# Two divisions of work moved off VectorE in a two-layer hybrid trunk: softmax scaling to ScalarE, the carried residual's gain and bias to GpSimd

## The chip, the cores and the metric

The kernel runs on one core of a Trainium2 chip. The metric is the device time of one execution in microseconds, median over runs. Of the core's engines, TensorE does matrix products into PSUM, VectorE (DVE in the profile), ScalarE (ACT) and GpSimd (POOL) do elementwise work, and SyncE (SP) issues most of the loads.

## What is computed

Two layers of a mixer with three parallel head groups over 256 tokens of width 2048, cut from the reference:

```python
h = x @ w_in                                     # one projection for all groups
y_a = chunk_band_attention(a_q, a_k, a_v, rel)   # 8 heads, softmax over a band of chunks
o_b = gla_chunk_recurrence(b_q, b_k, b_v, log_g) # 4 heads of gated linear attention
y_m = memory_attention(m_q, mk, mv)              # 4 heads, softmax over 256 memory tokens
y = concat([y_a * silu(a_z), rmsnorm(o_b) * silu(b_z), y_m * silu(m_z)])
x = layer_norm(ALPHA * x + y @ w_out, ln_g, ln_b)
# layer_norm: (x - mean) * rsqrt(var + eps) * ln_g + ln_b, over the 2048 columns
# softmax: exp(s - max) / sum
```

## The kernel before

All weights are streamed from memory, 512 KB at a time, and each product is made nearly exact in float32 by splitting both factors into a high and a low part: ScalarE casts a loaded tile to its high part (`high`, line 261, tile `wh`), VectorE subtracts that from the tile to get the low part (`low`, line 268, tile `wl`), and TensorE multiplies high by high, high by low and low by high (line 86). `take` runs casts three tiles and subtractions two tiles ahead of the tile that TensorE uses; `wh` has four buffers and `wl` three, so the two engines often wait for TensorE to let go of one.

The order of the work is set in two ways. TensorE and SyncE run in the order in which the program is written. ScalarE, VectorE and GpSimd are put in order by a scheduler ahead of the run, from its own estimates of when each step is ready; each engine then runs its list strictly in that order, waiting where it must. Casts and subtractions of weights carry a high priority there.

The heads are generators that run beside the weight stream. After every weight tile `tick` advances them, at most two heads at a time; a number yielded says after how many ticks the next step is written. So TensorE's part of a head (scores, transposes, products) stands at a fixed place between its weight tiles, whatever the other engines do.

- `a_head` (band attention, 8 heads a layer, in pairs): scores, bias, row maximum (line 718), exponential with the row sum as a by-product (line 720, ScalarE), reciprocal of the sum (line 722), then the scaling of the 128 x 384 scores in two pieces, 128 and 256 wide (line 724, in place, VectorE). Three ticks later TensorE transposes them (line 729).
- `m_head` (cross-attention, 4 heads a layer, in pairs 0 and 1, 2 and 3): the same with two pieces of 256; maximum at lines 753 and 754, exponential at 757, reciprocal at 760, scaling at 762, transposes two ticks later at 767.
- `gla` (the gated group) runs beside the first band heads. Its end is copied from PSUM (line 677), squared and summed (684), its root taken (504), scaled (690) and transposed (696).
- `norm_residual(l)` runs in layer 1 beside the stage of the gates. Between the layers `norm_between` leaves the normed values in `res` without gain and bias, since those are put on the transposed copy that feeds the products (line 828). `norm_residual` puts them on `res` itself, which is the residual of layer 1: for each of four column blocks SyncE loads a row of g and a row of b, spread over 128 partitions (line 841), and four operations of 128 x 512 multiply by g and add b for both token tiles (line 844). The rows lie in the same ring of eight scratch buffers as the scores, and SyncE's row loads stand among its weight loads.

In the stage of the gates each half of a group ends with `total` (lines 494 and 495), the gate's SiLU (1107), the product with the group's output (1109), differences of blocks (410 to 413) and splits (498 and 499).

GpSimd fills a few constants and issues small loads, among them the rows for the last norm (lines 797 and 798).

Of the kernel before, what the change touches and what calls it, by code (L numbers as in the profile page):

```python
# [13 lines left out]
ALU = mybir.AluOpType  # L14
# [38 lines left out]
def hybrid_trunk_kernel(  # L53
# [7 lines left out]
    pe, dve, act, pool, sp = nc.tensor, nc.vector, nc.scalar, nc.gpsimd, nc.sync  # L61
# [23 lines left out]
    def mm(o, l, r, start, stop):  # L85
        pe.matmul(o, l, r, start=start, stop=stop, skip_group_check=True)  # L86

    def scratch(shape, dtype=F32):
        return sc.tile(shape, dtype, name=nm("sc"), tag="sc")

    def small(shape, tag, bufs=1):
        return sm.tile(shape, F32, name=nm(tag), tag=tag, bufs=bufs)
# [33 lines left out]
    def banks(n):  # L126
        while len(free) < n:
            yield 1
        return [free.pop(0) for _ in range(n)]

    def release(*bs):
        free.extend(bs)
# [364 lines left out]
    def parts(hi, lo, src):  # L497
        act.copy(hi, src)  # L498
        dve.tensor_tensor(lo, src, hi.bitcast(F32), op=ALU.subtract)  # L499
# [205 lines left out]
    def a_head(h, load_bias, bias, q, k, asv, y):  # L705
        if h + 2 < 8:
            load_bias(h + 2)
        pb, = yield from banks(1)
        mm(ps[:, pb, 0:128], q[:, 0:128], k[:, 0:128], True, True)
        mm(ps[:, pb, 128:384], q[:, 128:256], k, True, True)  # L710
        s = scratch([P, 384])
        dve.scalar_tensor_tensor(s, ps[:, pb, :384], SCALE, bias[h], op0=ALU.mult, op1=ALU.add)
        release(pb)
        mx = small([P, 2], "mx", 4)
        zs = small([P, 2], "zs", 4)
        own = (slice(0, 128), slice(128, 384))
        for t in range(2):
            dve.tensor_reduce(mx[:, t:t + 1], s[:, own[t]], AX.X, ALU.max, negate=True)  # L718
        for t in range(2):
            act.activation(s[:, own[t]], s[:, own[t]], AF.Exp, bias=mx[:, t:t + 1], accum_out=zs[:, t:t + 1])  # L720
        yield 1
        dve.reciprocal(zs, zs)
        for t in range(2):
            dve.tensor_scalar(s[:, own[t]], s[:, own[t]], zs[:, t:t + 1], None, op0=ALU.mult)
        yield 3

        pt, = yield from banks(1)
        for i in range(3):
            pe.transpose(ps[:, pt, i * P:(i + 1) * P], s[:, i * P:(i + 1) * P], ident)  # L729
        pT = scratch([P, 384])  # L730
        act.copy(pT, ps[:, pt, :384])
        release(pt)
        yield 2
        po, = yield from banks(1)
        v0 = 528 + h * P
        mm(ps[:, po, 0:256], asv[:, 0, v0:v0 + P], pT[:, 0:256], True, False)
        mm(ps[:, po, 128:256], asv[:, 1, v0:v0 + P], pT[:, 256:384], False, True)
        act.copy(y, ps[:, po, :256])
        release(po)
        yield 1  # L740

    def m_head(h, q, mk, mv, y):
        pb, = yield from banks(1)
        for t in range(2):
            o = ps[:, pb, t * 256:(t + 1) * 256]
            qh, ql = (x[:, h, t * P:(t + 1) * P] for x in q)
            kh, kl = (x[:, h] for x in mk)
            mm(o, qh, kh, True, False)
            mm(o, ql, kh, False, False)
            mm(o, qh, kl, False, True)  # L750
        mx = small([P, 2], "mx", 4)
        zs = small([P, 2], "zs", 4)
        dve.tensor_reduce(mx, ps[:, pb].rearrange("p (t m) -> p t m", t=2), AX.X, ALU.max, negate=True)
        dve.tensor_scalar(mx, mx, SCALE, None, op0=ALU.mult)
        s = scratch([P, 2, 256])
        for t in range(2):
            act.activation(s[:, t], ps[:, pb, t * 256:(t + 1) * 256], AF.Exp, bias=mx[:, t:t + 1], scale=SCALE, accum_out=zs[:, t:t + 1])
        release(pb)
        yield 1
        dve.reciprocal(zs, zs)  # L760
        for t in range(2):
            dve.tensor_scalar(s[:, t], s[:, t], zs[:, t:t + 1], None, op0=ALU.mult)
        yield 2
        pt, = yield from banks(1)
        for m in range(2):
            for t in range(2):
                pe.transpose(ps[:, pt, m * 256 + t * P:m * 256 + (t + 1) * P], s[:, t, m * P:(m + 1) * P], ident)  # L767
        ph, pl = scratch([P, 2, 256], F32R), scratch([P, 2, 256], F32R)
        parts(ph, pl, ps[:, pt].rearrange("p (m t) -> p m t", m=2))
        release(pt)  # L770
        yield 2
        po, = yield from banks(1)
        for m in range(2):
            vh, vl = (x[:, m, h * P:(h + 1) * P] for x in mv)
            mm(ps[:, po, 0:256], vh, ph[:, m], m == 0, False)
            mm(ps[:, po, 0:256], vl, ph[:, m], False, False)
            mm(ps[:, po, 0:256], vh, pl[:, m], False, m == 1)
        act.copy(y, ps[:, po, :256])
        release(po)
        yield 1  # L780
# [3 lines left out]
    def columns(n):  # L784
        return slice(n * 512, (n + 1) * 512)
# [51 lines left out]
    def norm_residual(l):  # L837
        for n in range(4):
            for a, op in ((ln_g, ALU.mult), (ln_b, ALU.add)):
                row = scratch([P, 512])  # L840
                sp.dma_start(row, a[l:l + 1, columns(n)].to_broadcast([P, 512]))
                for t in range(2):
                    r = res[:, t, columns(n)]
                    dve.tensor_tensor(r, r, row, op=op)
            yield 6

    def norm_vectors():
# [118 lines left out]
    for l in range(L):  # L966
# [82 lines left out]
        def load_bias(h):  # L1049
            bias[h] = hd.tile([P, 384], F32, name=nm("bias"), tag="bias", bufs=3)  # L1050
            sp.dma_start(bias[h], relw[l, h])

        def add_heads(i):
            q, k = qk[i * 2:i * 2 + 2]
            gens.append([a_head(i * 4 + h, load_bias, bias, q[:, h], k[:, h], asv, yraw[1 + i][:, h]) for h in range(4)])
            waiting.extend(gens[-1])
# [27 lines left out]
        if l:  # L1084
            others = [norm_residual(l - 1)]
            beside(others)
        gens.append([m_head(h, q, mk, mv, yraw[3][:, h]) for h in range(4)])
        waiting.extend(gens[-1])

# [65 lines left out]
    with tc.manual_schedule(engines={mybir.EngineType.DVE}):  # L1155
# [6 lines left out]
        for h in range(2):  # L1162
            for kt in range(12, 16):
                moving(ps[:, 6 + h, :256], 1, [columned(v, kt % 2, True, h) for v in ws[kt // 2]], yq[3], kt % 4, kt == 12, kt == 15)
            r = res[:, 1, 1536 + h * 256:1792 + h * 256]
# [93 lines left out]
```

## Time and profile before

| | |
|---|---|
| median of 3 runs | 915.19 us (914.28 to 916.26) |
| profiled execution | 915.43 us, span 913.6 us |
| granted TensorE clock | 0.997 |
| busy: TensorE, VectorE, ScalarE, GpSimd | 904.7, 719.0, 552.4, 13.6 us |
| moved from memory | 193.16 MB read, 214 GB/s over the span |

Times in the profile are microseconds from the start of the span; in groups the mean is in nanoseconds. A row of a group ends with the idle time of the engine just before its instructions and with what ended most of it. In the timeline, consecutive instructions of a kind are merged into one row with their count. Consecutive operations on one engine overlap a little, so the spacing of starts is shorter than the time of one. TensorE's weight loads (PEld) run beside its products.

### The profile page before, as it was taken

How to read it: one execution, taken by the hardware profiler on the slowest of the kernel's cores; microseconds unless marked ns; L12 is line 12 of the kernel's file. 1: busy time of each engine (PE TensorE's matmuls, PEld its weight loads, DVE VectorE, ACT ScalarE, POOL GpSimd, SP SyncE). 2: the span in 40 equal slices, each digit the busy share in tenths (PEclk: the TensorE clock that was granted, in tenths of full speed). 3: DMA queues.
4: the chain of work that ended last, by engine and by line, in shares of the span. 5: the costliest groups of instructions: out<-in, count | busy, mean ns of one | idle time of the engine just before them, and what ended most of it. 6: DMA issues, size and time to landing. Idle time of an engine off the chain costs nothing.

```text
span 913.6 us, 14539 instructions
## 1 busy us (share of the span) xinstructions
PE 904.7 (99%) x5477; PEld 794.8 (87%) x5477; DVE 719.0 (79%) x997; ACT 552.4 (60%) x809; POOL 13.6 (1%) x32
## 2 busy tenths in 40 slices
PE   8999999999999999999999999999999999999997
PEld 6889999999888888788888899999988888888885
DVE  6597788788766777799978867886886778778996
ACT  6575555576576775655559755556756667565540
POOL 1000000000000000000000000000000000100000
PEclk9999999999999999999999999999999999999998
DMA  8858786776444455876765697666754565877652
GB/s 280 301 189 270 271 274 209 233 250 187 156 150 161 161 162 185 300 272 211 230 229 187 203 292 251 222 199 180 222 177 134 182 187 185 277 273 242 218 188 93
DMA packets 65014, 196.21 MB, mean 215 GB/s; under 512 B 7088, under 2 KB 10288, under 8 KB 64944
## 3 DMA queue, kind: packets, MB, share of 16 engines
q1 hardware_dynamic: 63920, 193.08, 64.2%
q0 software_dynamic: 1024, 2.21, 0.8%
q8 instruction: 43, 0.70, 0.3%
q14 instruction: 27, 0.22, 0.1%
HBM read 193.16 MB, written 2.10 MB: 214 GB/s over the span
## 4 chain that ended last, share of the span: by engine, by line
PE 94%; DVE 2%; DMA 1%; ACT 1%; issue 1%; SPq 0%; ACTq 0%; DVEq 0%
PE ps L86 93%; DMA raw<-w 1%; DVE wl L268 1%; PE ps L729 1%; PE ps L767 0%; ACT sz L828 0%; ACT wh L261 0%; DVE x L499 0%; SPq L352 0%; DVE res L812 0%; PE ps L696 0%; SPq L347 0%; DVE s L499 0%; ACT s L498 0%; DVE raw L410 0%
## 5 line engine op out<-in xcount | busy, mean ns | idle before, releaser
L268 DVE TENSOR_TENSOR wl<-raw,wh 128x1024 fp32r<-128x1024 f32 (+1 forms) x313 | 364.6, 1167 | 117.7 <-PE ps L86 78.4
L261 ACT CAST wh<-raw 128x1024 fp32r<-128x1024 f32 (+1 forms) x313 | 314.1, 1008 | 229.6 <-PE ps L86 123.6
L86 PE MATMUL ps<-x,wh 128*128 128x512 f32 x1408 | 445.4, 397 | 0.1
L86 PEld LDWEIGHTS ps<-x,wl 128*128 128x128 f32 x1408 | 264.4, 188 | 63.1 <-DVE wl L268 1.0
L86 PE MATMUL ps<-x,wl 128*128 128x256 f32 x1408 | 277.4, 278 | 0.5 <-DVE wl L268 0.5
L86 PE MATMUL ps<-wh,x 128*128 128x512 f32 (+1 forms) x852 | 247.4, 371 | 1.1 <-DVE sz L495 0.6
L86 PEld LDWEIGHTS ps<-x,wh 128*128 128x128 f32 x1408 | 219.2, 189 | 2.1 <-ACT sz L828 0.4
L86 PEld LDWEIGHTS ps<-wh,x 128*128 128x128 f32 x852 | 155.5, 189 | 21.1 <-ACT wh L358 1.1
L86 PE MATMUL ps<-wl,x 128*128 128x512 f32 (+1 forms) x426 | 157.8, 370 | 0.0
L86 PEld LDWEIGHTS ps<-wl,x 128*128 128x128 f32 x426 | 80.2, 188 | 10.7 <-DVE wl L359 0.4
L261 ACT CAST wh<-term 128x776 fp32r<-128x776 f32 (+1 forms) x39 | 36.0, 924 | 49.2 <-DVE term L260 42.0
L268 DVE TENSOR_TENSOR wl<-term,wh 128x776 fp32r<-128x776 f32 (+1 forms) x39 | 41.5, 1065 | 15.2 <-PE ps L86 14.6
L260 DVE TENSOR_TENSOR term<-term,term 128x776 f32<-128x776 f32 (+1 forms) x39 | 41.3, 1059 | 0.0
L86 PE MATMUL ps<-wh,s 128*128 128x512 f32 (+1 forms) x144 | 41.2, 367 | 0.0
L86 PEld LDWEIGHTS ps<-wh,s 128*128 128x128 f32 x144 | 25.8, 188 | 3.2
L86 PE MATMUL ps<-wl,s 128*128 128x512 f32 (+1 forms) x72 | 26.5, 368 | 0.0
L495 DVE SCALAR_TENSOR_TENSOR sz<-ps,sz 128x512 f32<-128x512 f32 x24 | 16.3, 684 | 4.3 <-ACT sz L494 3.5
L720 ACT ACTIVATE sc<-sc,mx 128x128 f32<-128x128 f32 (+1 forms) x32 | 14.2, 444 | 8.2 <-DVE mx L718 8.2
L86 PE MATMUL ps<-wh,sc 128*128 128x388 f32 x64 | 16.5, 338 | 0.0
L86 PEld LDWEIGHTS ps<-wl,s 128*128 128x128 f32 x72 | 13.5, 188 | 1.6
L1107 ACT ACTIVATE sz<-sz 128x512 f32<-128x512 f32 x16 | 10.1, 632 | 7.4 <-DVE sz L495 7.3
L86 PE MATMUL ps<-w,x 128*128 128x512 f32 (+1 forms) x72 | 14.4, 358 | 0.0
(221 smaller groups left out, 710.6 us busy)
## 6 DMA issues: line engine op xcount, KB each, us to landing
raw<-w SPq DMA_DIRECT2D x252, 512.0 KB, 4.3
raw<-w SPq DMA_DIRECT2D x64, 388.0 KB, 3.6
term<-w SPq DMA_DIRECT2D x24, 388.0 KB, 4.4
term<-w SPq DMA_DIRECT2D x15, 512.0 KB, 4.7
bias<-relw SPq DMA_DIRECT2D x16, 192.0 KB, 3.8
res<-xT SPq DMA_DIRECT2D x4, 512.0 KB, 6.4
res<-xn SPq DMA_DIRECT2D x4, 512.0 KB, 4.8
raw<-memT SPq DMA_DIRECT2D x4, 512.0 KB, 4.8
```

The lines of the kernel that those rows point to most:

```text
L86: pe.matmul(o, l, r, start=start, stop=stop, skip_group_check=True)
L260: in_order(dve.tensor_tensor(d.raw, d.raw, d.plus, op=ALU.add))
L261: act.copy(d.hi, d.raw)
L268: in_order(dve.tensor_tensor(d.lo, d.raw, d.hi.bitcast(F32), op=ALU.subtract))
L495: dve.scalar_tensor_tensor(dst, a, scale, dst, op0=ALU.mult, op1=ALU.add)
L720: act.activation(s[:, own[t]], s[:, own[t]], AF.Exp, bias=mx[:, t:t + 1], accum_out=zs[:, t:t + 1])
L729: pe.transpose(ps[:, pt, i * P:(i + 1) * P], s[:, i * P:(i + 1) * P], ident)
L1107: act.activation(sz, sz, AF.Silu)
```

## The change

Three edits. The scaling of the softmax, lines 724 and 762, becomes a ScalarE multiply by a per-partition factor, with the same operands in place; the reciprocals stay on VectorE. The gain and bias of the carried residual, line 844, go to GpSimd. Over the two layers that is 32 and 16 scalings, and 16 row operations of layer 1.

```diff
@@ a_head @@
         dve.reciprocal(zs, zs)
         for t in range(2):
-            dve.tensor_scalar(s[:, own[t]], s[:, own[t]], zs[:, t:t + 1], None, op0=ALU.mult)
+            act.mul(s[:, own[t]], s[:, own[t]], zs[:, t:t + 1])
         yield 3
@@ m_head @@
         dve.reciprocal(zs, zs)
         for t in range(2):
-            dve.tensor_scalar(s[:, t], s[:, t], zs[:, t:t + 1], None, op0=ALU.mult)
+            act.mul(s[:, t], s[:, t], zs[:, t:t + 1])
         yield 2
@@ norm_residual @@
                 for t in range(2):
                     r = res[:, t, columns(n)]
-                    dve.tensor_tensor(r, r, row, op=op)
+                    pool.tensor_tensor(r, r, row, op=op)
             yield 6
```

The lists of TensorE and SyncE are the same before and after. The scheduler places the moved steps, and shifts some of their neighbours, on the other three engines.

On ScalarE, at cross-attention heads 0 and 1 of layer 0 (`sc_3037` is head 0's scores, `sc_3050` head 1's, `zs` their sums; `wh` are weight casts, `s_3253` and `s_3254` splits of differences):

```order
 L261 CAST wh_3081<-raw_2980 128x1024
 L757 ACTIVATE sc_3050,zs_3047<-ps,mx_3046 128x256 x2
+L762 ACTIVATE sc_3037<-sc_3037,zs_3034 128x256 x2
 L498 CAST s_3253<-raw_3255 128x512
 L498 CAST s_3254<-raw_3255 128x256 x2
 L261 CAST wh_3103<-raw_3009 128x1024
+L762 ACTIVATE sc_3050<-sc_3050,zs_3047 128x256 x2
 L261 CAST wh_3146<-raw_3057 128x1024
 L494 ACTIVATE sz_3125<-ps 128x512
```

Two scalings of head 0 now stand ahead of the splits; the two of head 1 stand behind the splits and one more weight cast.

On ScalarE, at heads 2 and 3 of layer 0 (`sc_3276` and `sc_3289`):

```order
 L757 ACTIVATE sc_3289,zs_3286<-ps,mx_3285 128x256 x2
 L261 CAST wh_3320<-raw_3208 128x1024
+L762 ACTIVATE sc_3276<-sc_3276,zs_3273 128x256 x2
+L762 ACTIVATE sc_3289<-sc_3289,zs_3286 128x256 x2
 L261 CAST wh_3342<-raw_3230 128x1024
 L498 CAST s_3514<-raw_3516 128x512
```

Here all four scalings stand together, behind one weight cast that was there before; the next weight cast and the splits stand behind them. Layer 1 has both pieces in the same form.

On VectorE, in layer 1, around the second block of columns (`sc_7285` and `sc_7289` are the rows of g and b, `yr_5981` the gated group's output, `mx` the maxima of cross-attention heads 0 and 1):

```order
 L268 TENSOR_TENSOR wl_7301<-raw_7183,wh_7263 128x1024
-L844 TENSOR_TENSOR res<-res,sc_7285 128x512 x2
-L844 TENSOR_TENSOR res<-res,sc_7289 128x512 x2
 L268 TENSOR_TENSOR wl_7330<-raw_7213,wh_7299 128x1024
 L495 SCALAR_TENSOR_TENSOR sz_7321<-ps,sz_7321 128x512
 L268 TENSOR_TENSOR wl_7378<-raw_7245,wh_7328 128x1024
+L1109 TENSOR_TENSOR yr_5981<-sz_7321,yr_5981 128x512
 L753 TENSOR_REDUCE mx_7356<-ps 128x2
 L753 TENSOR_REDUCE mx_7369<-ps 128x2
-L1109 TENSOR_TENSOR yr_5981<-sz_7321,yr_5981 128x512
+L410 TENSOR_TENSOR raw_7586<-yr_5981 128x256
```

The four row operations leave VectorE for GpSimd's list, and the product of line 1109 moves ahead of the two maxima, as it stands in layer 0. GpSimd's list gains the sixteen operations, in four groups of four; the last group stands among the loads of the last norm's rows.

## The prediction

> **What bounds the kernel now.** The engine shares and the chain's shares on the page come first.
>
> ```profile
> PE 904.7 (99%) x5477; PEld 794.8 (87%) x5477; DVE 719.0 (79%) x997; ACT 552.4 (60%) x809; POOL 13.6 (1%) x32
> ...
> PE 94%; DVE 2%; DMA 1%; ACT 1%; issue 1%; SPq 0%; ACTq 0%; DVEq 0%
> ```
>
> TensorE is busy for 904.7 of 913.6 us and carries 94% of the chain. Busy time alone could hide waits, so the second view is the list of waits, for TensorE alone; these are its two longest.
>
> ```profile
> PE ps L86 <- DVE wh L328: 1.5, 1, 1.5
> PE ps L86 <- DVE sz L495: 0.6, 1, 0.6
> ```
>
> The 1.5 is at the kernel's start. In the stages that the change touches TensorE waits for nobody, so there is nothing there to win by making VectorE lighter. The program carries its own test of that: layer 1's gate stage is layer 0's plus the sixteen row operations of line 844. The chain in order of time and the busy time by stage show both between the same two groups of transposes:
>
> ```profile
> 307.50 0.87 PE ps L767 x8
> ...
> 330.71 0.87 PE ps L767 x8
> ...
> 756.46 0.87 PE ps L767 x8
> ...
> 779.67 0.87 PE ps L767 x8
> ```
>
> ```profile
> 307.50:330.70 23.20, 23.20 (x146) 20.71 (x145) 16.84 (x30) 16.12 (x27) 0.00 (x0) 1.00 0.51 159
> 756.50:779.70 23.20, 23.20 (x146) 20.71 (x145) 19.62 (x35) 17.09 (x29) 0.00 (x0) 1.00 0.58 182
> ```
>
> VectorE (third busy figure) has 2.8 us more to do in layer 1, and TensorE takes 23.21 us in both. Everything in layer 1 lies 448.96 us (756.46 - 307.50) after its twin in layer 0; I use that shift below.
>
> So the question is only whether the moved work makes TensorE wait where it did not.
>
> **What is moved, and what it costs each engine.**
>
> ```profile
> L844 DVE TENSOR_TENSOR res<-res,sc 128x512 f32<-128x512 f32 x16 | 10.4, 686 | 3.8 <-DMA sc<-ln_g 2.9 <-DMA sc<-ln_b 0.9
> ...
> L724 DVE TENSOR_SCALAR sc<-sc,zs 128x256 f32<-128x256 f32 x16 | 5.5, 346 | 0.0
> ...
> L762 DVE TENSOR_SCALAR sc<-sc,zs 128x256 f32<-128x256 f32 x16 | 4.6, 346 | 0.0
> L724 DVE TENSOR_SCALAR sc<-sc,zs 128x128 f32<-128x128 f32 x16 | 4.5, 282 | 0.2
> ```
>
> VectorE loses 10.4 + 5.5 + 4.6 + 4.5 = 25.0 us. By the above that is worth 0 on the path.
>
> ScalarE gains 48 multiplies with a per-partition factor. Its nearest row is the softmax's exponential, also in place in SBUF with one per-partition operand:
>
> ```profile
> L720 ACT ACTIVATE sc<-sc,mx 128x256 f32<-128x256 f32 x16 | 7.9, 495 | 0.0
> ```
>
> ```profile
> 196.91 0.50 ACT L720 ACTIVATE sc<-sc,mx 128x256 f32<-128x256 f32 x1
> 197.31 0.19 ACT L720 ACTIVATION_READ_ACCUMULATOR sc<-sc,mx 128x1 f32 x1
> ```
>
> One 256-wide operation lasts 0.50 us and the next instruction starts 0.40 after it, so two in a row end 0.90 after the first starts. I take 0.40 a piece (0.30 for 128 wide); 0.33 to 0.50 are the ends. The sum over the kernel, about 18 us, lies in ScalarE's idle time. What matters is where in its queue the multiplies stand, because TensorE's transposes read their result at once, with their places in TensorE's own queue unchanged.
>
> **Cross-attention heads 0 and 1: the term of the sum.** Layer 0, timelines of ScalarE, VectorE and TensorE's weight loads:
>
> ```profile
> 305.31 1.24 ACT L498 CAST s<-raw 128x512 fp32r<-128x512 f32 x3
> 306.43 2.01 ACT L261 CAST wh<-raw 128x1024 fp32r<-128x1024 f32 x2
> 308.33 0.61 ACT L494 ACTIVATE sz<-ps 128x512 f32<-128x512 f32 x1
> ```
>
> ```profile
> 303.60 0.17 DVE L760 RECIPROCAL zs<-zs 128x2 f32<-128x2 f32 x1 [0.29 <-ACT sc L757]
> ...
> 305.46 0.17 DVE L760 RECIPROCAL zs<-zs 128x2 f32<-128x2 f32 x1 [0.84 <-ACT sc L757]
> ...
> 306.68 0.61 DVE L762 TENSOR_SCALAR sc<-sc,zs 128x256 f32<-128x256 f32 x2
> ```
>
> ```profile
> 307.24 0.90 PEld L767 LDWEIGHTS ps<-ident,sc 128*128 128x128 f32 x8
> ```
>
> Today head 1's division ends at 307.29 and the eight transposes, 0.11 apart, begin loading at 307.24; the sixth, the first that needs the last division, loads at about 307.8. The new order puts head 0's two multiplies at the front, then the three casts of line 498, then one weight cast, and only then head 1's two. Head 0 starts at 305.31 (its reciprocal is there at 303.77) and takes 0.80, to 306.11. The three casts take 306.43 - 305.31 = 1.12, to 307.23: head 0 is in time. The weight cast takes (308.33 - 306.43) / 2 = 0.95, to 308.18; it is a tile that TensorE needs only several us later. Head 1's multiplies then end at 308.18 + 0.90 = 309.08. TensorE, waiting from 307.8, resumes at 309.1: **1.3 us** lost. With 0.33 or 0.50 a piece it is 1.0 to 1.6. Nothing gives it back, since TensorE is the bound afterwards.
>
> Layer 1 has the same order, without the row operations that set it apart, so by the shift it loses 1.3 us as well.
>
> **Heads 2 and 3** have their four multiplies together behind one weight cast:
>
> ```profile
> 327.81 2.00 ACT L261 CAST wh<-raw 128x1024 fp32r<-128x1024 f32 x2
> ```
>
> ```profile
> 327.96 0.17 DVE L760 RECIPROCAL zs<-zs 128x2 f32<-128x2 f32 x1 [0.74 <-ACT sc L757]
> ```
>
> ```profile
> 330.54 1.03 PE L767 MATMUL ps<-ident,sc 128*128 128x128 f32 x8
> ```
>
> The cast ends at 328.76, the four multiplies at 328.76 + 3 x 0.40 + 0.50 = 330.46; the last one's transposes come at 330.54 + 0.5. No cost, 0.6 us in hand.
>
> **The eight band-attention heads of each layer** wait longer for their transposes, but ScalarE's copies of the gated group's output now stand behind one pair's four multiplies (1.40 us), and behind them the root of the norm has moved past one weight cast (0.95) and one copy like that of line 494 above (0.6): 2.95 us in all. VectorE's scaling and the transposes that read it:
>
> ```profile
> 259.74 1.29 DVE L690 TENSOR_TENSOR sc<-sc,rr 128x512 f32<-128x512 f32 x2
> ```
>
> ```profile
> 264.16 1.04 PE L696 MATMUL ps<-ident,sc 128*128 128x128 f32 x8
> ```
>
> The second scaling moves from 261.03 to 263.98; its transposes start half a group in, at 264.6. No cost, but that cover is thin: 0.6 us more on ScalarE would begin to show, in both layers.
>
> **GpSimd's sixteen row operations.** The trace has no two-input operation on GpSimd. Its memset of the same tile:
>
> ```profile
> L551 POOL MEMSET sc<- 128x512 f32 x2 | 1.1, 538 | 307.9 <-DVE wl L268 307.9
> ```
>
> 0.54 us is the low end; three such passes (two reads and a write), 1.6 us, the high one; I take 1.1, midway. The Trainium skill (GPSIMD Engine Reference, Engine selection) speaks against this change: it sends elementwise work on a tile to VectorE, with GpSimd about twice as slow on two inputs; by that rule against the 686 ns row a piece costs some 1.4 us (an estimate from that page), and the sum below stays. Four pieces per pair of rows (one of g, one of b) take 4.4 us. When the pairs come, when line 923 first reads the residual after them, when SyncE issues the third pair's load, and when line 942 reads the last norm's rows:
>
> ```profile
> L844 DVE TENSOR_TENSOR res<-res,sc x16: 677/685/694, 723.9 to 788.2; 128x512 f32<-128x512 f32 x16
> ```
>
> ```profile
> L923 DVE SCALAR_TENSOR_TENSOR res<-res,ps x2: 679/680/680, 390.2 to 835.5; 128x512 f32<-128x512 f32 x2
> ```
>
> ```profile
> 759.61 0.42 SPq L841 DMA_DIRECT2D sc<-ln_g  x1
> ```
>
> ```profile
> L942 DVE TENSOR_TENSOR res<-res,sc x2: 682/682/683, 875.2 to 877.5; 128x512 f32<-128x512 f32 x2
> ```
>
> The four pairs spread over 723.9 to 788.2, 21 us apart, and the residual is read at 835.5, over 40 us later: their length is hidden. Three queues get a new wait. SyncE's third load now waits for GpSimd's second pair to free the row buffer, with weight loads queued behind it; that pair, begun at 742.6, is over 10 us before 759.6. GpSimd's own last row operations stand between the loads of the last norm's rows and delay those by at most 4 pieces, 6 us, of some 80. And ScalarE's multiplies wait for VectorE's reciprocals, with the weight casts behind them; each reciprocal stands before or right behind one weight subtraction, and those casts are two tiles ahead of TensorE. All three are costed at 0; without the cover each would cost what it waits.
>
> **Sum.** The profiled run took 915.43 us (span 913.6 and 1.8 around it), 0.03% from the median of 915.19. Plus 1.3 + 1.3: **918.0**. What a measurement of this kernel can tell from no change is 0.2%, 1.8 us.
>
> **Rivals.**
>
> *GpSimd holds VectorE off (28%).* If an operation with two SBUF inputs cannot run on VectorE while GpSimd runs one, layer 1 gets later than its twin. The row pair that collides, as it lands today, and the twin's operations:
>
> ```profile
> 742.57 1.29 DVE L844 TENSOR_TENSOR res<-res,sc 128x512 f32<-128x512 f32 x2 [1.49 <-DMA sc<-ln_g]
> 744.57 1.29 DVE L844 TENSOR_TENSOR res<-res,sc 128x512 f32<-128x512 f32 x2 [0.70 <-DMA sc<-ln_b]
> ```
>
> ```profile
> 295.01 1.23 DVE L268 TENSOR_TENSOR wl<-raw,wh 128x1024 fp32r<-128x1024 f32 x1 [2.89 <-PE ps L86]
> ...
> 298.88 0.69 DVE L1109 TENSOR_TENSOR yr<-sz,yr 128x512 f32<-128x512 f32 x1
> ```
>
> GpSimd works from 742.57 to 744.8; VectorE's subtraction, due at 743.97, waits to 744.8 and ends at 746.0; turn about, the next subtraction ends at 748.3 and line 1109, due at 747.84, starts at 748.3 or, behind GpSimd's last piece, at 749.4. That is 0.5 to 1.6 us late, and the maxima, the exponentials and the multiplies follow it: 918.5 to 919.6. No row of this trace has both engines in such operations. The Trainium skill (SBUF — State Buffer, Who interferes with whom) states just this lock; no run so far shows it.
>
> *The delay is given back between the layers (9%).* Not slower. The chain there leaves TensorE:
>
> ```profile
> 474.40 5.22 DMA raw<-w
> ```
>
> ```profile
> 470.00:502.00 32.00, 31.92 (x179) 27.00 (x178) 27.83 (x44) 25.66 (x44) 0.00 (x0) 1.00 0.63 209
> ```
>
> If TensorE really waits for that load, and the load does not move with TensorE, layer 0's 1.3 vanishes: 916.7, within 0.2%. It decides only where TensorE idles there; it was idle for 0.08 us, so this is unlikely.
>
> *The multiplies come in time (7%).* The order does not hold as read, or ScalarE runs 1.3 us ahead of its old times: 915.4.
>
> *GpSimd is far slower than 1.6 us a piece (4%)* and, holding VectorE off, starves the weight subtractions too: from about 3 us a piece each pair would outlast the two tiles (of eight in 23.2 us: 5.8 us) that VectorE is ahead, 4 pairs by some 2 us each: 918 + 8 = 926.
>
> *VectorE did pace TensorE (2%).* The one wait for it, 0.6, goes and more: below 913.6.
>
> **Numbers.** The forecast itself has 50%. Slower: 0.44 of it, the first rival's 28 and the starved case's 4, 0.76. Same: 0.06 + 0.09 + 0.07 = 0.22. Faster 0.02. The range runs from the given-back case less half a us, 916.2, to the first rival's upper end and as much as the runs scatter, 920.4; it leaves out the in-time, starved and faster cases, 13%, and some tails.
>
> **What would show it.** TensorE should wait for ScalarE's line 762 twice, once in each layer, 1.0 to 1.6 us, at the first pair of cross-attention heads and nowhere else; the gap between line 767's two groups in the layers should stay 23.2. Longer subtractions on VectorE while GpSimd is busy, and a longer wait in layer 1 than in layer 0, would speak for the first rival. No wait on line 762 would make the prediction wrong, as would a wait on line 690 or on a weight tile.

## The result, and the profile after

The changed kernel takes 920.79 us (median of 4 runs, 919.5 to 922.3) against 915.73 for the kernel before beside it: a ratio of 1.0059 with an interval of 1.0047 to 1.0072, so 5.1 us slower. The prediction said 918.0, slower by 2.6. The profiled execution took 921.09 us, span 919.3.

The engine shares and the chain's shares first:

```profile
PE 906.9 (99%) x5477; PEld 795.2 (86%) x5477; DVE 709.7 (77%) x933; ACT 569.7 (62%) x857; POOL 40.7 (4%) x48
...
PE 95%; ACT 2%; DVE 1%; DMA 1%; SPq 0%; issue 0%; ACTq 0%; DVEq 0%
```

VectorE's busy time fell by only 9.3 of the 25.0 us that were taken off it; ScalarE's grew by 17.3, and its part of the chain from 1% to 2%. TensorE's busy time grew by 2.2 us with the same instructions, a first hint at a slower clock and no more than that: it also moves by a microsecond or two between kernels whose clock holds (906.6 us in the run with the softmax alone, below). Next, what TensorE's weight loads waited for, the longest of its list, and one that is new:

```profile
PEld ps L767 <- ACT sc L762: 4.7, 6, 2.2
...
PEld ps L729 <- ACT yr L599: 0.2, 1, 0.2
```

The wait on line 762 that was forecast is there, at cross-attention heads 0 and 1 in both layers. The timeline of the weight loads shows that the two layers differ:

```profile
308.59 0.14 PEld L767 LDWEIGHTS ps<-ident,sc 128*128 128x128 f32 x1 [1.06 <-ACT sc L762]
308.99 0.31 PEld L767 LDWEIGHTS ps<-ident,sc 128*128 128x128 f32 x3 [0.26 <-ACT sc L762]
...
757.83 0.14 PEld L767 LDWEIGHTS ps<-ident,sc 128*128 128x128 f32 x1 [0.65 <-ACT sc L762]
758.23 0.31 PEld L767 LDWEIGHTS ps<-ident,sc 128*128 128x128 f32 x3 [0.26 <-ACT sc L762]
760.71 0.14 PEld L767 LDWEIGHTS ps<-ident,sc 128*128 128x128 f32 x1 [2.17 <-ACT sc L762]
761.11 0.31 PEld L767 LDWEIGHTS ps<-ident,sc 128*128 128x128 f32 x3 [0.26 <-ACT sc L762]
```

The waits in brackets add up to 1.32 us in layer 0 and 3.34 in layer 1. The chain in order of time gives the same stages as the rows shown of before: the last group of band transposes, then TensorE's weight products behind the waits, then the transposes of heads 2 and 3, in each layer.

```profile
284.40 0.66 PE ps L729 x6
...
309.54 22.34 PE ps L86 x136
331.88 0.87 PE ps L767 x8
...
734.45 0.66 PE ps L729 x6
...
761.66 23.90 PE ps L86 x136
785.56 0.87 PE ps L767 x8
```

In the kernel before, the same chain has these rows:

```profile
284.56 0.66 PE ps L729 x6
...
308.37 22.33 PE ps L86 x136
...
733.52 0.66 PE ps L729 x6
...
757.33 22.34 PE ps L86 x136
```

From the band transposes to the next weight products it is 23.81 us in both layers before (308.37 - 284.56, 757.33 - 733.52). After, it is 25.14 in layer 0 and 27.21 in layer 1: 1.33 and 3.40 us lost. Then, in layer 1 alone, the same 136 products take 23.90 us in place of 22.34: another 1.56. The clock granted to TensorE in that stretch, by stretches of 1 us (the figure in the place before the DMA share):

```profile
762.00:763.00 1.00, 1.00 (x6) 0.86 (x5) 0.48 (x1) 1.00 (x3) 0.00 (x0) 0.74 0.40 53
763.00:764.00 1.00, 1.00 (x5) 0.90 (x4) 1.00 (x3) 0.98 (x2) 0.00 (x0) 0.50 0.81 319
...
765.00:766.00 1.00, 1.00 (x5) 0.90 (x4) 0.58 (x1) 0.77 (x2) 0.00 (x0) 0.56 1.01 215
```

The clock falls to 0.50 near 762.5, 1.4 us after the last of the waits in brackets, and is back near 765.9: 3.4 us at half speed. Before and behind these rows it is 1.00. TensorE's lag behind the kernel before, read off the chain at the same rows, adds up so:

| stretch | lag gained, us |
|---|---|
| start, up to the last band transposes of layer 0 | -0.16 |
| heads 0 and 1, layer 0 | +1.33 |
| heads 2 and 3, layer 0 | 0 |
| from there to layer 1's first band heads | -0.46 |
| first band transposes of layer 1 (wait on line 599) | +0.2 |
| heads 0 and 1, layer 1 | +3.40 |
| the 136 products behind them | +1.56 |
| heads 2 and 3, layer 1, and the rest | -0.1 to -0.2 |
| sum (span 919.3 - 913.6) | +5.7 |

The -0.46 does not come from the change. It belongs to this one execution of the kernel before, whose weight loads wait 0.4 us for line 828 and 0.3 us for a subtraction between 470 and 505 us. The kernel before with only the later transposes, a run below, loses nothing in layer 0, has neither wait and gains nearly as much: its chain shows the last band transposes of the two layers 448.53 us apart (448.81 with the rows alone), where the kernel before has 448.96 (733.52 - 284.56):

```profile
284.62 0.66 PE ps L729 x6
...
733.15 0.66 PE ps L729 x6
```

What made layer 1's wait longer is seen on VectorE. Its timeline in layer 1, and GpSimd's in the same stretch:

```profile
744.90 1.37 DVE L268 TENSOR_TENSOR wl<-raw,wh 128x1024 fp32r<-128x1024 f32 x1 [2.89 <-PE ps L86]
746.24 0.69 DVE L495 SCALAR_TENSOR_TENSOR sz<-ps,sz 128x512 f32<-128x512 f32 x1
747.63 2.12 DVE L268 TENSOR_TENSOR wl<-raw,wh 128x1024 fp32r<-128x1024 f32 x1 [0.70 <-PE ps L86]
749.68 1.77 DVE L1109 TENSOR_TENSOR yr<-sz,yr 128x512 f32<-128x512 f32 x1
```

```profile
743.90 7.00 POOL L844 TENSOR_TENSOR res<-res,sc 128x512 f32<-128x512 f32 x4 [12.01 <-DMA sc<-ln_g]
```

GpSimd's four row operations last from 743.90 to 750.90. In that time VectorE's two subtractions last 1.37 and 2.12 us where 1.23 was usual, and the product of line 1109 1.77 where it was 0.69. The first subtraction's 0.14 is absorbed, since VectorE waits 0.70 us for TensorE before the second; the other two make 0.89 + 1.08 = 1.97 us, all ahead of the maxima of heads 0 and 1. Line 495, which reads one of its two operands from PSUM, keeps its 0.69.

### The profile page after: what moved, and what is told of

The parts are those of the page before. It is cut to its first block, busy times and chain, and to the rows that moved or that the text cites. A ratio compares the mean times of both kernels' runs of the same rounds, so it can differ in the third digit from the quotient of the medians.

```text
span 919.3 us, 14552 instructions
## 1 busy us (share of the span) xinstructions
PE 906.9 (99%) x5477; PEld 795.2 (86%) x5477; DVE 709.7 (77%) x933; ACT 569.7 (62%) x857; POOL 40.7 (4%) x48
## 4 chain that ended last, share of the span: by engine, by line
PE 95%; ACT 2%; DVE 1%; DMA 1%; SPq 0%; issue 0%; ACTq 0%; DVEq 0%
PE ps L86 93%; DMA raw<-w 1%; PE ps L729 1%; DVE wl L268 0%; ACT wh L261 0%; PE ps L825 0%; ACT sc L757 0%; ACT sc L762 0%; PE ps L767 0%; ACT L757 0%; DVE mx L753 0%; DVE yr L1109 0%; ACT s L498 0%; SPq L352 0%; PE ps L696 0%
## 5 line engine op out<-in xcount | busy, mean ns | idle before, releaser
L268 DVE TENSOR_TENSOR wl<-raw,wh 128x1024 fp32r<-128x1024 f32 (+1 forms) x313 | 369.8, 1184 | 133.5 <-PE ps L86 78.2
L844 POOL TENSOR_TENSOR res<-res,sc 128x512 f32<-128x512 f32 x16 | 27.4, 1739 | 184.9 <-DMA sc<-ln_g 184.9
L1109 DVE TENSOR_TENSOR yr<-sz,yr 128x512 f32<-128x512 f32 x16 | 14.6, 912 | 4.3 <-ACT sz L1107 4.3
```

Source lines behind the costliest of these rows:

```text
L268: in_order(dve.tensor_tensor(d.lo, d.raw, d.hi.bitcast(F32), op=ALU.subtract))
L844: pool.tensor_tensor(r, r, row, op=op)
L1109: dve.tensor_tensor(yraw[i][:, j:j + 2], sz, yraw[i][:, j:j + 2], op=ALU.mult)
```

## The experiments

The theory when they began: the loss has three parts, (a) ScalarE's strict order at heads 0 and 1, 1.3 us in each layer; (b) GpSimd's row operations holding off VectorE's operations on two operands in SBUF, some 2 us more in layer 1; (c) TensorE's clock, which halves after the long wait that (a) and (b) make together. The chief rivals: (b) is only VectorE's changed order, and (c) has nothing to do with the wait. For all runs with a profile the same measure is used: from the start of the last band transposes (line 729) to the start of the next 136 weight products, less the 23.81 us of the kernel before.

| kernel | layer 0, lost | layer 1, lost | longest line 268 of 313, us | ratio to the kernel before |
|---|---|---|---|---|
| before | 0 | 0 | 1.23 | |
| changed | 1.33 | 3.40 | 2.32 | 1.0059 [1.0047, 1.0072] |
| softmax alone | 1.33 | 2.59 | 1.23 | 1.0063 [1.0047, 1.0079] |
| cross-attention's softmax alone | 1.34 | 1.42 | 1.23 | 1.0042 [1.0030, 1.0054] |
| rows alone | 0 | 1.35 | 2.37 | 1.0019 [1.0011, 1.0028] |
| memsets for the rows | 1.33 | 1.36 | 1.23 | 1.0031 [1.0019, 1.0043] |
| copies for the rows | 1.34 | 1.35 | 1.67 | profile only |

### The softmax alone

```diff
-                    pool.tensor_tensor(r, r, row, op=op)
+                    dve.tensor_tensor(r, r, row, op=op)
```

> The softmax's multiplies on ScalarE, the row operations of line 844 back on VectorE. Theory (the loss is three things: ScalarE's order at heads 0 and 1, GpSimd holding VectorE off in layer 1, and TensorE's granted clock that halves after the long wait there): layer 0 waits 1.3 us on line 762 as in the changed kernel; in layer 1 the maxima of heads 0 and 1 come some 0.7 us later than in layer 0 because VectorE has the row pair before them, so there the wait is 1.5 to 2.3 us in pieces, none over 1.6; the granted clock stays at 1.00 behind it; some 0.5 is given back between the layers. In all 2.2 to 3.2 us over the kernel before. Rival A (GpSimd's part does nothing, the whole loss is the softmax's): layer 1's wait is 3.4 us, the clock falls to 0.5 behind it, and all 5.1 us stay. Rival B (any wait of 2 us in all pulls the clock down): 1.5 us more than the theory, 3.7 to 4.7.

It took 920.4 us (919.28 to 923.01) against 914.99. The profiled execution, one of the short ones at 919.54, has the two waits, and the chain shows layer 1's:

```profile
734.66 0.66 PE ps L729 x6
...
761.06 22.20 PE ps L86 x135
```

761.06 - 734.66 = 26.40, so 2.59 us are lost: rival A's 3.4 is out, and the theory's 2.3 was a little low. VectorE's timeline shows what is late in layer 1:

```profile
745.09 2.50 DVE L844 TENSOR_TENSOR res<-res,sc 128x512 f32<-128x512 f32 x4 [2.86 <-DMA sc<-ln_g]
```

VectorE stands for 2.86 us before a row load that has not landed, with the subtraction of 747.50 behind it, and passes that on to the maxima. So the row operations cost layer 1 something on either engine once ScalarE does the scaling. In this execution the clock behind the waits (0.97, 1.20 and 0.26 us) stays at 1.00, so rival B, that any wait of 2 us in all pulls it down, is out too. The span is 3.9 us longer, 0.7 beyond the theory's range; the median is 5.4 us longer. The two longest executions, 921.97 and 923.01, have a mean clock of 0.995 where the three shortest have 0.997 to 0.999, but that of 921.26 has 0.998, so the clock is not all of the spread. By the medians the softmax alone is as slow as the whole change (5.4 and 5.1 us), so rival A's total is met where its wait is not; no profile shows one of the longer executions. The low means fit a clock that falls in some executions and not in others, and the runs with copies below take that up.

### The rows alone

```diff
-                    dve.tensor_tensor(r, r, row, op=op)
+                    pool.tensor_tensor(r, r, row, op=op)
```

(lines 724 and 762 stay on VectorE)

> Only the row operations of line 844 on GpSimd; the softmax's multiplies on VectorE as before. Theory (an operation of VectorE with two operands in SBUF slows or stops while GpSimd runs one): line 268 takes 2 us and more in place of 1.23 and line 1109 1.7 in place of 0.69 near 743 to 751 us; VectorE's chain to head 1's multiply comes 1.6 us later, to about 758.1 against TensorE's need at 756.8, so TensorE waits 1.0 to 1.5 us there, in layer 1 alone, and the clock stays at 1.00. In all 1.0 to 1.5 us over the kernel before, no wait in layer 0. Rival A (no lock: those operations were late for another reason): 0, within 0.5 us of the kernel before, and line 268 stays at 1.23. Rival B (GpSimd's work alone makes the clock fall): some 1.5 us with the clock at 0.5 near 762 but no wait ahead of it.

916.74 us against 914.99, 1.7 us more [1.0, 2.6]. VectorE's timeline, from the stretch of the row pair to head 1's scaling, and TensorE's wait for it:

```profile
743.88 2.37 DVE L268 TENSOR_TENSOR wl<-raw,wh 128x1024 fp32r<-128x1024 f32 x1 [2.89 <-PE ps L86]
...
746.77 1.71 DVE L268 TENSOR_TENSOR wl<-raw,wh 128x1024 fp32r<-128x1024 f32 x1
748.40 1.78 DVE L1109 TENSOR_TENSOR yr<-sz,yr 128x512 f32<-128x512 f32 x1
...
757.38 0.61 DVE L762 TENSOR_SCALAR sc<-sc,zs 128x256 f32<-128x256 f32 x2
```

```profile
757.78 0.57 PEld L767 LDWEIGHTS ps<-ident,sc 128*128 128x128 f32 x4 [1.20 <-DVE sc L762]
```

The hold is there without any change to the softmax, and costs 1.35 us in layer 1, within the theory's 1.0 to 1.5 (the median's 1.7 is above it); layer 0 loses nothing and the clock stays at 1.00 behind the wait. Both rivals fall. The hold is not only on operations with two tiles: line 724's scalings, with one tile and a per-partition factor, last 1.12, 1.39 and 1.12 us where they run against a row operation near 727 to 730 us, and 0.28 and 0.35 elsewhere.

### Memsets, then copies, for the rows

```diff
-                    pool.tensor_tensor(r, r, row, op=op)
+                    for _ in range(3):
+                        pool.memset(row, 0.0)
```

> The changed kernel with each of GpSimd's row operations replaced by three memsets of the row tile, about as long (3 x 0.54 us); the norm's gain and bias are left out of the residual. GpSimd is as busy at the same places but reads nothing. Theory (it is GpSimd's reading beside VectorE's that costs): line 268 stays at 1.23 us and line 1109 at 0.69, layer 1's wait is 1.3 to 1.6 us as in layer 0, the clock stays at 1.00, in all 2.0 to 2.8 us over the kernel before. Rival A (any access of GpSimd to SBUF holds VectorE off): wait 3.4, clock 0.5, 5.1 us. Rival B (the sixteen operations taken off VectorE only changed its order for the worse): also 5.1, with line 268 at 1.23.

918.21 us against 914.99. With GpSimd busy for as long at the same place (in the stretch of the second pair, from 743.27 to 750.1, with 0.9 us of waiting for the second row in it) but only writing, no subtraction lasts longer than 1.23 us:

```profile
L268 DVE TENSOR_TENSOR wl<-raw,wh x313: 941/1219/1229, 12.2 to 885.1; 128x1024 fp32r<-128x1024 f32 x137, 128x776 fp32r<-128x776 f32 x20
...
734.07 0.66 PE ps L729 x6
...
759.24 22.34 PE ps L86 x136
```

The longest in the changed kernel is 2.316. Layer 1 loses 1.36 us, as layer 0 does, and the products behind it take 22.34 us, at full clock. Both rivals fall. The total, 3.2 us, is over the 2.0 to 2.8 expected; the profiled execution has some 1.1 us of that far behind the stage, from 874.71 on, where the chain leaves TensorE for a weight load; what delays that load was not tried.

```diff
-                    pool.tensor_tensor(r, r, row, op=op)
+                    pool.tensor_copy(row, row)
```

> The changed kernel with each of GpSimd's row operations replaced by a copy of the row tile onto itself: one operand read and one written, where it had two read. The norm's gain and bias are left out of the residual. Theory in its wide form (any reading by GpSimd holds VectorE's two-operand operations off): some of line 268's operations near 725 and 744 us last 1.5 us or more, as in the changed kernel (up to 2.32). Theory in its narrow form (only GpSimd's operations with two operands do): line 268's longest stays at 1.23 us, as with the memsets, and layer 1's wait on line 762 is 1.3 to 1.6 us.

With one operand read, the hold is back. VectorE's and GpSimd's timelines at the third pair:

```profile
764.58 1.67 DVE L268 TENSOR_TENSOR wl<-raw,wh 128x1024 fp32r<-128x1024 f32 x1
766.92 1.63 DVE L268 TENSOR_TENSOR wl<-raw,wh 128x1024 fp32r<-128x1024 f32 x1
```

```profile
764.56 0.61 POOL L844 COPY sc<-sc 128x512 f32<-128x512 f32 x1 [8.41 <-DMA sc<-ln_g]
765.65 3.37 POOL L844 COPY sc<-sc 128x512 f32<-128x512 f32 x3 [0.48 <-DMA sc<-ln_b]
```

The subtraction takes 0.44 us longer beside a copy of 0.61, and the three copies take 3.37 together where three times 0.61 would be 1.8: each side waits for the other. The times say how: the two take turns. The first copy runs from 764.56 to 765.17, the subtraction that begins just behind it ends 1.08 later, at 766.25; the next copy, begun meanwhile at 765.65, ends 0.47 after that, and so on. The changed kernel keeps the same order: GpSimd's third row operation, alone at 1.28 us, ends at 748.67, the subtraction begun at 747.63 ends at 749.76, the fourth row operation at 750.90, line 1109 at 751.45.

So the wide form holds: it is GpSimd's reading, of one operand or two. It was expected to lengthen subtractions near 725 and 744 us as well, and there it did not. The two did meet, but the subtraction had begun first (at 726.78 and 745.50), kept its 1.23 us, and the copy waited:

```profile
727.19 1.29 POOL L844 COPY sc<-sc 128x512 f32<-128x512 f32 x1 [1.03 <-DMA sc<-ln_b]
```

That is why heads 0 and 1 lose only 1.35 us here. The Trainium skill (SBUF — State Buffer, Who interferes with whom) states this rule, that a VectorE instruction with two SBUF inputs contends with a GpSimd instruction that reads SBUF and not with one that only writes; by that rule, the three runs agree.

### The transposes one weight tile later

```diff
@@ m_head @@
             act.mul(s[:, t], s[:, t], zs[:, t:t + 1])
-        yield 2
+        yield 3
```

> The changed kernel with each cross-attention head's transposes put one weight tile (2.8 us of TensorE) later. Theory (the loss is nothing but the two waits on line 762 and the clock's fall behind the longer): layer 0's wait goes, layer 1's 3.4 shrinks to 0 to 0.9, the clock stays at 1.00, in all 0 to +1.0 us against the kernel before, with line 268 still stretched near the row pairs. Rival A (GpSimd's hold on VectorE starves the weight tiles too): waits on line 268's output take the place, +2 and more. Rival B (the clock falls with GpSimd's activity, not with the wait): +1.5 at least, with the clock at 0.5 near 762.

915.5 us against 914.99: ratio 1.0006 [0.9998, 1.0015]. All the moved work stays moved, and nine tenths of the loss is gone. Two rows of what TensorE's weight loads waited for are left of it:

```profile
PEld ps L767 <- ACT sc L762: 0.3, 1, 0.3
...
PEld ps L86 <- DVE sc L499: 0.4, 1, 0.4
```

Line 268's longest is still 2.38 us, so GpSimd's hold goes on, and both waits, in layer 1 alone, come from it: ahead of the second, line 1109's product, begun at 763.91 beside a row operation, lasts 1.83 us, and line 499 is late behind it. So the hold is cheap once the transposes are not due at once, not free. Both rivals fall: the waits on line 268's output make 1.5 us in all, 1.3 in the kernel before, and the clock stays at 1.00. The control, the kernel before with the same one-word edit:

> The kernel before, with the cross-attention's transposes put one weight tile later and nothing else changed: the control for the repaired kernel, which stood 0.5 us over the kernel before (ratio 1.0006). Theory (the later place in itself costs and wins nothing where nobody waits): within 0.5 us of the kernel before, so what the repair won came from the waits. Rival (the later place is in itself slower or faster by a microsecond): 1 us or more to either side.

915.2 us against 915.29, ratio 0.9997 [0.9988, 1.0006]. The later place is worth nothing by itself, so what the repair won was the waits and what follows them. No version here beats the kernel before: TensorE bounds it, and relief of VectorE buys nothing.

### Which of the two softmaxes, and the changed kernel again

```diff
-            dve.tensor_scalar(s[:, t], s[:, t], zs[:, t:t + 1], None, op0=ALU.mult)
+            act.mul(s[:, t], s[:, t], zs[:, t:t + 1])
```

(line 762 alone)

> Only the cross-attention's multiplies (line 762) on ScalarE; the band heads' (line 724) and the row operations as before. Theory (all of the softmax's loss is at heads 0 and 1): 1.3 us of wait in layer 0, 2.6 in layer 1 as with both softmaxes moved, 0.5 given back between the layers, 3.4 us over the kernel before where the clock holds and 5 to 6 where it falls, so a median of 3.4 to 5.5; no wait on line 599's copy at the first band pair of layer 1. Rival (line 724's moves carry a good part of the loss): 1.5 to 2.5 us over the kernel before, with shorter waits on line 762.

918.42 us against 915.28: 3.1 us, between the rival's 1.5 to 2.5 and the theory's 3.4 to 5.5. Layer 1 loses 1.42, not 2.6: here VectorE waits only 1.10 us for the row load, and the maxima start 14.53 us after the band transposes, not 15.71 as with the softmax alone: 1.18 us apart, where the two losses are 1.17 apart. So the extra wait of the softmax alone needs line 724's moves too. The two traces show the likely path, which no run tried by itself: line 724's multiplies put ScalarE's SiLU (line 1107) 0.88 us later, with it line 499's split and the subtraction behind that (0.80), and SyncE, which reloads that subtraction's buffer before it issues the row load, issues the row load 0.79 later. In both kernels layer 1's order on ScalarE differs from layer 0's (three multiplies stand behind the weight cast, not two), so that 1.42 lies near 1.34 is partly chance. A further 0.6 us is lost in layer 1 on line 499, behind VectorE's last row pair. The wait on line 599 is gone, as expected.

> The changed kernel once more, for the spread of its time. Theory (the granted clock falls in some executions and not in others, by where the wait lies in the throttle's own rhythm): two groups of times, near 919.3 and near 921 to 922, and the executions of the second group show the lower mean clock (0.995 to 0.996 against 0.998 to 0.999); waits on line 762 as before, 1.3 us in layer 0 and 3.4 in layer 1. Rival (the fall belongs to the wait each time): one group, all with the lower clock.

Six executions took 919.56, 919.57, 920.44, 920.52, 920.68 and 923.66 us, median 920.48, ratio 1.0062 [1.0049, 1.0075]. The two clean groups did not come, though the shortest two have a mean clock of 0.997 and the longest 0.994. The profiled one is that of 920.44 us. Its clock falls as TensorE resumes near 760.3, not 1.4 us later, and is back near 763.5:

```profile
760.00:761.00 1.00, 0.72 (x3) 0.51 (x4) 1.00 (x1) 1.00 (x3) 0.00 (x0) 0.54 0.94 373
...
763.00:764.00 1.00, 1.00 (x6) 0.78 (x5) 0.97 (x2) 0.98 (x2) 0.00 (x0) 0.76 1.01 399
```

In layer 1 it loses 3.40 us up to the products (761.58 - 734.37 - 23.81) of which 0.36 is the slower transposes (1.31 us from the first to the products, 0.95 in the first profile), and the products take 23.26 us, 0.92 over the kernel before: 1.3 us to the clock in all. TensorE's idle time ahead of it is a single one of 1.93 us.

An execution in which it did not fall would take 921.09 - 1.56 = 919.5 by the first profile's sum, which is where the shortest executions lie; no profile shows one of these, so that is argued and not shown.

### Waits of a chosen length

```diff
@@ m_head, on the kernel before @@
-        yield 2
+        yield dose(act, s)
...
+DOSE = [0, 1, 0, 2, 0, 4, 0, 7]
+
+def dose(act, s):
+    for _ in range(DOSE.pop(0)):
+        act.copy(s, s)
+    return 2
```

> The kernel before, with copies of the softmax's tile in place by ScalarE (about 0.6 us each) ahead of the transposes of the cross-attention heads 1 and 3: 1 and 2 of them in layer 0, 4 and 7 in layer 1; with what stands between them on ScalarE that makes four waits of TensorE between about 0.5 and 8 us. Theory (a long idle time of TensorE pulls its granted clock down afterwards, a short one does not): clock 1.00 behind waits under 1.5 us, 0.5 for some 3.5 us behind waits of 3.5 us and more, either between. Rival (the fall has nothing to do with the wait): the clock stays at 1.00 behind the long waits, or falls behind short ones as often.

> As the run before it, with 6 and 4 copies in layer 0 and 2 and 9 in layer 1, so that long and short waits change places. Theory: 0.5 for some 3.5 us behind the waits of 3.5 us and more, wherever they are; 1.00 behind those under 1.5. Rival (the place, not the length, decides): the fall comes at heads 0 and 1 of layer 1 again, whatever the wait there.

> As the earlier runs with copies ahead of the transposes of heads 1 and 3, now 2 and 3 of them in layer 0 and 1 and 4 in layer 1, for waits of TensorE between about 1 and 3.5 us. Those seen so far: no fall of the clock behind waits of 0.89 us and less, 0.5 behind waits of 2.84 us and more. Theory: the bound lies between 1 and 2.84 us and moves with the phase of the throttle, so of the waits of 1.5 to 2.8 us some are followed by 0.5 and some not, or at once for a part of it. Rival (a fixed length decides): all waits over some length are followed by it and none under.

> The run before it once more, the same kernel. Theory (phase decides in the middle range): at one of the waits of 1 to 2.8 us at least the clock behaves otherwise than in the first execution, or the fall's length differs by 0.5 us and more. Rival (length alone decides): the same falls at the same places, as long.

The copies' line number is 1266. All waits lie between the transposes of the two heads of a pair. TensorE's timeline gives each, as the row of the second head's transposes with the idle time ahead of it; at full clock those four take 0.66 us. One row of the second run:

```profile
774.00 1.12 PE L767 MATMUL ps<-ident,sc 128*128 128x128 f32 x4 [2.84 <-ACT sc L1266]
```

and three of the third and fourth, which are the same kernel:

```profile
335.60 0.66 PE L767 MATMUL ps<-ident,sc 128*128 128x128 f32 x4 [2.84 <-ACT sc L1266]
...
789.85 0.66 PE L767 MATMUL ps<-ident,sc 128*128 128x128 f32 x4 [3.36 <-ACT sc L1266]
```

```profile
789.20 1.11 PE L767 MATMUL ps<-ident,sc 128*128 128x128 f32 x4 [3.36 <-ACT sc L1266]
```

| wait, us (run) | clock behind it |
|---|---|
| 0.89 (first) | 1.00 |
| 1.01 and 1.04 (fourth, third) | 1.00 |
| 1.60 (third and fourth) | 1.00 |
| 2.84 (third and fourth) | 1.00 |
| 2.84 (second) | 0.50 at once, back 3.4 us after TensorE resumed |
| 3.36 (third) | 1.00 for 1.3 us, then 0.50 for 3.4 |
| 3.36 (fourth) | 0.50 at once, back after 2.7 us |
| 3.49 (second) | 0.50 at once, back after 3.2 us |
| 5.31, 6.36 (first) | 0.50 at once, back after 3.7 and 3.2 us |
| 6.61, 6.84 (second) | 0.50 at once, back after 5.9 and 5.2 us |

The fall belongs to the wait: it came behind every one of 3.36 us and more, at either pair of heads and in either layer, and behind none of 1.60 or less. Between, the same length, 2.84 us, did it once and not twice, a single wait of 1.93 us did it in the changed kernel's second profile, and at 3.36 us two executions of one kernel differ in when it began: length alone does not decide. The rivals, that the place decides or a fixed length, fall.

What phase means is in the trace's record of the clock: in every profile here, all changes of the clock lie a whole number of steps of 3.41 us apart (in the first run at 760.61, 767.44, 791.33 and 798.16: two, seven and two steps). Cut into these steps, two of the three waits of 2.84 us look like this, in the second run and in the third (TensorE's busy time stands behind the length of the stretch, the clock before the DMA share):

```profile
770.58:773.99 3.41, 0.58 (x6) 0.34 (x4) 3.18 (x6) 3.41 (x6) 0.00 (x0) 1.00 0.44 154
773.99:777.41 3.42, 3.41 (x12) 3.02 (x13) 1.86 (x4) 2.83 (x4) 0.00 (x0) 0.50 0.88 275
```

```profile
330.38:333.79 3.41, 2.38 (x16) 1.91 (x14) 3.41 (x8) 3.41 (x8) 0.00 (x0) 1.00 0.23 80
333.79:337.21 3.42, 1.61 (x10) 1.48 (x11) 2.20 (x4) 2.34 (x4) 0.00 (x0) 1.00 0.78 247
337.21:340.62 3.41, 3.41 (x21) 2.97 (x21) 1.81 (x3) 1.75 (x3) 0.00 (x0) 1.00 0.13 50
```

In the one the whole wait falls into one step, and the next step is at 0.50; in the other it is split over two, as it is in the fourth run. Behind the waits of all these profiles, the clock fell after steps with 0 to 1.69 us of busy time and held after steps with 1.56 and more; the two ranges overlap a little, so busy time is not quite what is counted. It came back at the end of the first step in which TensorE was busy for 2.73 us or more; steps with 2.53 and less did not bring it back. At the very end of the kernels, where the work is of other kinds, this does not hold.

The kernels with copies have VectorE do the row operations, so GpSimd has no part in the fall. The Trainium skill (TensorE: Matmul & The Clock Gate, Part 1) puts both changes of the clock down to an activity window of about 3.4 us that runs freely, beside the kernel; by that rule, the steps of 3.41 us, the shift of the start and the lengths agree, but it lets the clock fall after an idle window, and here it fell behind waits of 2.84 and 1.93 us, with TensorE busy for part of the window.

## Why the prediction was right or wrong

- **TensorE is the bound, and relief of VectorE is worth 0: right.** The kernel with all moves and later transposes is at 1.0006.
- **ScalarE's multiplies at 0.40 us apiece: right.** Those of 256 last 0.51 us and start 0.41 apart.
- **Layer 0, 1.3 us at heads 0 and 1: right.** It measured 1.33 in every kernel that moves line 762, through the row that the order named: three splits and one weight cast ahead of head 1.
- **"Layer 1 has the same order ... by the shift it loses 1.3 us as well": wrong, and this is the step that failed.** The wait measured 3.40, with 1.56 more behind it in clock. The order alone does cost 1.3 there: with memsets in place of the rows it is 1.36. The rest, 2.0, is GpSimd's hold on VectorE. (Left on VectorE, with the softmax moved, the row operations cost layer 1 most of that too, 2.59 in all, by their load's late landing.) The forecast took the row operations out of layer 1's stage as if they left nothing there. The first rival named this mechanism and the very pair of rows, at 28%.
- **The rival's price, 0.5 to 1.6 us, was low:** the hold cost 2.0. It rested on 1.1 us a piece; alone a piece takes 1.28, and taking turns stretched the pair to 7.00 us, not 4.4, so that the second subtraction waited 0.89 and line 1109 another 1.08. The row of line 844 now, with the least, the median and the most of a piece in nanoseconds:

```profile
L844 POOL TENSOR_TENSOR res<-res,sc x16: 1279/1386/2379, 724.9 to 795.7; 128x512 f32<-128x512 f32 x16
```

The least is a piece alone, the most one that VectorE holds off in turn; the group's mean is 1.74 us.
- **The clock: not foreseen.** No term or rival had it, though the prediction's own sum made TensorE idle. It took 1.56 us in the profiled execution and 1.3 in the second profile; without it the profiled time would have been 919.5, inside the range.
- **"Nothing gives it back": right, as far as the traces show.** The changed kernel comes to layer 1 with 0.46 us less than layer 0's loss, but the control that loses nothing in layer 0 gains nearly as much (0.43): it is the kernel before, in its profiled execution, that waits there. The forecast read 0.08 us of idle time off TensorE's products; its weight loads waited 0.4 and 0.3 in the same stretch.
- **Heads 2 and 3 at 0: right. Band heads at 0: nearly,** 0.2 us at one wait on line 599, which is gone when line 724 stays on VectorE.
- **New waits of SyncE and GpSimd at 0: right** in the changed kernel; TensorE waits for neither; what GpSimd cost came through VectorE.

By the parts: the forecast's two waits, 1.33 + 1.36, less the 0.46 that the kernel before lost by itself, plus the hold's 2.04, the clock's 1.56 and 0.2, make 6.0 us, and the execution's earlier start and end of 0.3 leave the 5.7 of the span.

## What to carry to other kernels

Before moving an elementwise step with operands in SBUF to GpSimd, look up in the timeline which of VectorE's operations on operands in SBUF will lie beside it, and let the two take turns: whichever begins second ends its own length after the other. Two-operand operations and line 724's scalings were held, row maxima and an operation with an operand in PSUM were not. Where a held one stands in a chain that ends at the bounding engine, the move costs. Price a wait of the bounding matrix engine by its length: up to 1.6 us it cost itself here, from 1.9 us on it could cost 1.3 to 1.6 us more in clock. A result due at once can be made due one tile later; here that had no price of its own and took out nine tenths of the loss.

## What the runs showed of the hardware that was not expected

- VectorE's subtraction of two tiles in SBUF, 1.23 us alone, lasted up to 2.38 beside GpSimd's two-operand operations, 1.67 beside its copies and 1.23 beside its memsets; line 1109's product, 0.69 alone, up to 3.20 (at 794.38 in the changed kernel, against two row operations), and line 724's scaling, 0.35 alone, up to 1.39. Line 495 with an operand in PSUM (0.69) and the row maxima of line 718 (0.28 and 0.41) kept their time.
- GpSimd's 128 x 512 two-operand operation took 1.28 us alone and up to 2.38 beside VectorE, a copy 0.61 and up to 1.60, a memset 0.53.
- TensorE's granted clock fell to 0.50 behind idle times of 1.93 us (a single one in one profile, with 0.45 us shortly before it in another), 2.84 (once in three) and 3.36 to 6.84 (always). All changes of the clock in a profile lay whole steps of 3.41 us apart. It came back 2.7 to 5.9 us after TensorE resumed, and cost 1.56 us in the changed kernel.
